# Two groups' small products in one run on TensorE, with four buffers each for their matrices and powers

## The chip, the cores and the metric

The kernel runs on one core of a Trainium2 chip. Its time is device microseconds of one execution, and the number that counts is the median of several. The core has five engines with a queue each: TensorE (PE in the profile; its weight loads have a row of their own, PEld), VectorE (DVE), ScalarE (ACT), GpSimd (POOL) and SyncE (SP, which here only issues transfers). Each engine works through its queue in order.

## The reference, cut to what matters

Two layers on 256 tokens of width 2048, in fp32. Each layer is a token mixer, a cross-attention to 256 memory tokens, and an MLP with a squared ReLU. Layer 1's mixer is a state space layer: 128 channel groups of 16 channels, each driving 64 complex states.

```
lam_bar = exp(lam * dt)
b_bar = ((lam_bar - 1.0) / lam)[..., None] * bmat
bu = einsum('gpc,bsgc->sbgp', b_bar, u)
_, states = associative_scan(combine, (a, bu), axis=0)
y = einsum('gcp,sbgp->bsgc', cmat, states).real + d_skip * u
...
def squared_relu_mlp(h, w_up, w_down):
    return jnp.square(jax.nn.relu(h @ w_up)) @ w_down
```

## The kernel before

**Large matmuls.** Weights come as tiles of 128 x 1024 floats through SyncE's queue (`wload`, L127) into four buffers `wraw`, with a fifth in the first MLP. ScalarE casts each to a high part `whi` (L103) and VectorE subtracts to get the low part `wlo` (L104); each of these has three buffers. TensorE multiplies high by high and low activations and low by high activations. In the MLP's up projection (`gemm_feat`, L174 and L179) a tile is eight matmuls of 512 columns and eight of 256; in the down projection (`gemm_hid`, L814, L815, L817) it is twelve of 512. The first MLP (`mlp`, layer 0) has four blocks of 32 up tiles and 32 down tiles.

**The state space preparation.** What the state space layer needs of its parameters doesn't depend on tokens. `ssm_prep` works it out during the first MLP. It puts small steps on a list `side`; every second tile, `tick` takes one step and traces it under `later(200)`, which lowers the priority of its instructions by 200 against the matmuls around them, so they stand later in the queues of the engines than where they were traced. The first steps work out the powers of the poles (`power`, tiles `pw`), transpose them (`spread`, L1026, to `T1` and `T2`) and write eight rows of factors to DRAM (`row`, `Ld`, L1014). Then come 32 "quads" of four channel groups, in three steps each:

- `quad(q)` loads the quad's matrices `bcq` (GpSimd) and half of its factors `lb` (SyncE, L1062) and makes the input matrix `bb` (L1077 to L1079), in one of two buffers.
- `quad_q(q)` loads the other half of `lb`, from `Ld`, makes the products of the output matrices and the powers, `qt` (L1087 to L1089, two buffers), sends them to DRAM (`Qd`), and multiplies `bb` by `qt` on TensorE: four matmuls, one per channel group, each with 32 columns of weights and 128 moving columns, into 32 partitions each of one PSUM tile `kp` (L1100). A matmul in fp32 leaves two records in the trace. ScalarE (L1104) and VectorE (L1105) copy `kp` to `kd`, of which GpSimd has cleared the first part (L1103), and GpSimd sends `kd` to DRAM in four transfers (`Kd`, L1108).
- `quad_p(q)` multiplies the factors to `po` (two buffers) and sends it to DRAM (`Pd`, L1122).

The four products carry a priority that makes up for their order, so that all four have the same one:

```
for g in range(4):
    with self.tc.high_priority(offset=g):
        nc.tensor.matmul(kp[32 * g:32 * g + 32], bb[:, g], qt[:, 0:T, g, :], start=True, stop=True,
                         skip_group_check=True)
```

**The next stage.** `s5` reads `Pd`, `Qd` and `Kd` back. It has runs of small matmuls of the same shape as the products above: `own` (L1215) and `outputs` (L1263, followed by L1269).

**Activation tiles.** `act` has two buffers of 128 x 8192 floats. In the first MLP one holds its input `hT`; the other, which held the attention's output, is idle until the norm of the next layer takes it in the last block (`nxt.start`).

Of the kernel before, what the change touches and what calls it, by code (L numbers as in the profile page):

```python
# [9 lines left out]
F32 = mybir.dt.float32  # L10
# [3 lines left out]
ALU = mybir.AluOpType  # L14
AX = mybir.AxisListType

P = 128
D = 2048
S = 256
KT = D // P  # L20
# [10 lines left out]
G = 128  # L31
T = 8
# [6 lines left out]
class Trunk:  # L39
# [590 lines left out]
    def mlp(self, x, layer, cur, nxt):  # L630
# [3 lines left out]
        with tc.tile_pool(name="ml", bufs=4, reuse_waits="tile") as mp:  # L634
            r2 = mp.tile([P, 32 if layer else 56], F32, name="r2", bufs=1)[:, 0:2]
            ws = lambda: mp.tile([P, KB * NB], F32, name="ws", bufs=4)
# [272 lines left out]
    def ssm_prep(self, pool):  # L909
# [14 lines left out]
        self.Qd = mk("Qd", [2, 64, 2, 4 * P])  # L924
        self.Kd = mk("Kd", [16, NL, 2, 4, 16])
        Ld = self.dram.tile([T, G, 2, 64], F32, name="Ld")
# [7 lines left out]
        F = pool.tile([P, 2, G], F32, name="F", bufs=1)  # L934
        e = {}

        def cmul(orr, oi, ar, ai, br, bi):
# [9 lines left out]
        def poles():  # L947
# [5 lines left out]
            nc.gpsimd.memset(T2[:, 0, :], 0.0)  # L953
            e["bb"] = [pool.tile([P, 4, 2, 16], F32, name=f"bb{i}") for i in range(2)]
            for b in e["bb"]:
                nc.gpsimd.memset(b[:, :, 1], 0.0)
            lr, li = pool.tile(W, F32, name="lr", tag="w0"), pool.tile(W, F32, name="li", tag="w1")
            ld = pool.tile([P, 1], F32, name="ld")
# [8 lines left out]
        def place(k):  # L967

            if k % 4 == 1:
                e["p4"] = pool.tile([P, 4, 2, P], F32, name="pw", tag="lb", bufs=2)  # L970
            e["pw"].append(tuple(e["p4"][:, (k - 1) % 4, i] for i in range(2)))
            return e["pw"][k]
# [77 lines left out]
        def inputs(q):  # L1050
            e["bcq", q] = bcq = pool.tile([P, 4, 4, 16], F32, name="bcq", bufs=3)
            nc.gpsimd.dma_start(out=bcq, in_=a["b_bc"][q])

        def factors(q, i):

            if i == 0:
                e["lb", q] = pool.tile([P, 2, 4, 2, 64], F32, name="lb", bufs=2)
            b = a["b_pc"][q]
            src = (bass.AP(tensor=b.tensor, offset=b.offset, ap=[[0, T], [8 * 64, 16], [1, 8 * 64]]),
                   bass.AP(tensor=Ld.tensor, offset=Ld.offset + q * 8 * 64, ap=[[G * 2 * 64, T], [0, 16], [1, 8 * 64]]))  # L1060
            with self.tc.issue_after(self.fed):
                nc.sync.dma_start(out=e["lb", q][:, i], in_=src[i])  # L1062

        def quad(q):
            factors(q, 0)
            bcq = e.pop(("bcq", q))
# [4 lines left out]
            B1, C2, B2, C1 = (bcq[:, i] for i in range(4))  # L1071
            bb = e["bb"][q % 2]
            tq = pool.tile([P, 4, T + 1, 16], F32, name="tq")
# [17 lines left out]
        def quad_q(q):  # L1091
            factors(q, 1)
            bcq, bb, tq = e[q]
            qt = pool.tile([P, T + 1, 4, 16], F32, name="qt", bufs=2)
            times(qt.rearrange("p w g c -> p g w c"), tq, T + 1, q, bcq[:, 3], bcq[:, 1])
            nc.gpsimd.dma_start(out=self.Qd[q // 2][q % 2].rearrange("p r n -> r p n"), in_=qt[:, 1:])
            kp = self.ps([P, T, 16])
            for g in range(4):
                with self.tc.high_priority(offset=g):
                    nc.tensor.matmul(kp[32 * g:32 * g + 32], bb[:, g], qt[:, 0:T, g, :], start=True, stop=True,  # L1100
                                     skip_group_check=True)
            kd = pool.tile([P, NL, 16], F32, name="kd", bufs=2)
            nc.gpsimd.memset(kd[:, 0:T - 1, :], 0.0)  # L1103
            nc.scalar.copy(out=kd[:, T:, :], in_=kp[:, 1:, :])  # L1104
            v.scalar_tensor_tensor(out=kd[:, T - 1, :], in0=eye, scalar=dsk[:, q:q + 1], in1=kp[:, 0, :],  # L1105
                                   op0=ALU.mult, op1=ALU.add)
            for t in range(4):
                nc.gpsimd.dma_start(out=self.Kd[q // 2][:, :, q % 2, t], in_=kd[32 * t:32 * t + 16])  # L1108

        def quad_p(q):  # L1110

            tq, lb = e.pop(q)[2], e.pop(("lb", q))
            bt = lb[:, 0]
            po = pool.tile([P, 4, 2, 64], F32, name="po", bufs=2)
            tmp = tq.rearrange("p a b c -> p (a b c)")[:, 0:512].rearrange("p (t r s) -> p t r s", t=4, r=2)
# [5 lines left out]
            v.tensor_tensor(out=po[:, :, 1], in0=po[:, :, 1], in1=tmp[:, :, 1], op=ALU.add)  # L1121
            nc.gpsimd.dma_start(out=self.Pd[q // 2][:, q % 2], in_=po.rearrange("p t r s -> p t (r s)"))  # L1122

        sd = self.side
# [3 lines left out]
        sd += [lambda k=k: power(k) for k in range(5, T + 1)]  # L1128
        sd += [lambda: spread(5), lambda: (last(), inputs(0))]
        for q in range(G // 4):  # L1130
# [6 lines left out]
    def s5(self, x, cur, nxt):  # L1137
# [3 lines left out]
        with tc.tile_pool(name="s5", bufs=2, reuse_waits="tile") as sp:  # L1141
# [110 lines left out]
            def outputs(n, half):  # L1252
# [4 lines left out]
                for i in (2 * half, 2 * half + 1):  # L1257
                    dq = ahead.pop(("dq", n, i)).rearrange("p (j l t c) -> p l t j c", j=T, l=2, t=4)
                    qq = ahead.pop(("qq", n, i))
# [283 lines left out]
```

## Time and profile before

| | us |
|---|---|
| median of 3 runs | 2790.95 |
| lowest, highest | 2790.82, 2792.07 |
| the profiled execution | 2789.63 |
| its span, first to last instruction | 2787.9 |
| TensorE matmuls busy | 2767.1 |
| VectorE busy | 1984.8 |
| ScalarE busy | 1396.2 |
| GpSimd busy | 234.4 |

The profile is of one execution, which is 1.3 us shorter than the median. Between its time and its span lie 1.7 us. Busy times are unions of the records of an engine; matmuls overlap each other in the records, since the end of one is modelled, so the distance from one start to the next tells more of TensorE than the busy share does.

### The profile page before, as it was taken

To read this page: it belongs to the slowest core of one execution; us is meant where nothing else is said; L and a number is where in the kernel's file an instruction comes from. 1 tells how busy PE (TensorE), PEld (TensorE's weight loads), DVE (VectorE), ACT (ScalarE), POOL (GpSimd) and SP (SyncE) were. 2 spreads that over 40 slices of the span, in tenths; PEclk is the share of its full clock that TensorE was granted. 3 is DMA by queue.
4 is the path that set the end of the run, shared out by engine and by line. 5 is a ranking of instruction groups with operands and counts; after the bars stand their busy time and mean duration, and the time that the engine had idled before them with its cause. 6 is when DMAs were issued, how large, how long until landed. Compare 5 with 4: busy or idle time off the path is not lost. (4 is left out here: it accounts for less than half of the span.)

```text
span 2787.9 us, 39690 instructions
## 1 busy us (share of the span) xinstructions
PE 2767.1 (99%) x15020; PEld 2331.6 (84%) x15020; DVE 1984.8 (71%) x2740; ACT 1396.2 (50%) x1805; POOL 234.4 (8%) x435
## 2 busy tenths in 40 slices
PE   9999999999999999999999999999999999999998
PEld 7888888888888888888887888888888888888887
DVE  6865756778978778787567657557776767667665
ACT  6545544554534434444556445445554545445454
POOL 0100000001022222221213100000000000000000
PEclk9999999999999999999999999999999999999999
DMA  8766655557788888887879767564556566565655
GB/s 294 232 209 217 200 179 181 175 158 244 211 260 260 255 259 262 257 259 226 240 242 270 217 199 239 176 191 159 179 158 216 170 212 204 164 221 167 213 187 158
DMA packets 196223, 593.76 MB, mean 213 GB/s; under 512 B 45120, under 2 KB 47216, under 8 KB 195520
## 3 DMA queue, kind: packets, MB, share of 16 engines
q1 hardware_dynamic: 151728, 531.17, 60.7%
q0 software_dynamic: 43776, 59.01, 7.8%
q8 instruction: 117, 1.92, 0.3%
q10 hardware_dynamic: 528, 1.06, 0.1%
q14 instruction: 74, 0.61, 0.1%
HBM read 567.51 MB, written 23.46 MB: 212 GB/s over the span
## 5 line engine op out<-in xcount | busy, mean ns | idle before, releaser
L104 DVE TENSOR_TENSOR wlo<-wraw,whi 128x1024 fp32r<-128x1024 f32 (+1 forms) x893 | 1085.9, 1221 | 490.4 <-ACT whi L103 484.8
L103 ACT CAST whi<-wraw 128x1024 fp32r<-128x1024 f32 (+1 forms) x893 | 937.3, 1052 | 857.0 <-PE acc L731 204.5
L174 PE MATMUL acc<-act,whi 128*128 128x512 f32 x3072 | 742.4, 392 | 0.6 <-ACT whi L103 0.6
L174 PEld LDWEIGHTS acc<-act,whi 128*128 128x128 f32 x3072 | 562.7, 188 | 111.5 <-issue 2.6
L179 PEld LDWEIGHTS acc<-act,wlo 128*128 128x128 f32 x3072 | 394.9, 191 | 18.6 <-DVE wlo L104 2.9
L179 PE MATMUL acc<-act,wlo 128*128 128x256 f32 x3072 | 403.9, 283 | 1.9 <-DVE wlo L104 1.5
L159 PE MATMUL acc<-whi,act 128*128 128x512 f32 x1472 | 369.8, 393 | 6.2 <-ACT whi L103 5.4
L159 PEld LDWEIGHTS acc<-whi,act 128*128 128x128 f32 x1472 | 275.1, 189 | 64.0 <-ACT whi L103 5.4
L731 PE MATMUL acc<-whi,act 128*128 128x512 f32 x864 | 233.0, 392 | 0.0
L815 PE MATMUL acc<-whi,hl 128*128 128x512 f32 x544 | 213.3, 392 | 0.0
L814 PE MATMUL acc<-whi,hh 128*128 128x512 f32 x544 | 212.7, 391 | 0.0
L159 PE MATMUL acc<-wlo,act 128*128 128x512 f32 x736 | 197.9, 391 | 0.0
L731 PEld LDWEIGHTS acc<-whi,act 128*128 128x128 f32 x864 | 160.3, 188 | 36.5 <-ACT ends L763 1.9
L159 PEld LDWEIGHTS acc<-wlo,act 128*128 128x128 f32 x736 | 138.6, 188 | 28.9
L731 PE MATMUL acc<-whi,hh 128*128 128x512 f32 x378 | 148.4, 393 | 0.0
L731 PE MATMUL acc<-whi,hl 128*128 128x512 f32 x378 | 147.1, 389 | 0.0
L817 PE MATMUL acc<-wlo,hh 128*128 128x512 f32 x544 | 145.9, 390 | 0.0
L731 PE MATMUL acc<-wlo,act 128*128 128x512 f32 x432 | 133.1, 390 | 0.0
L815 PEld LDWEIGHTS acc<-whi,hl 128*128 128x128 f32 x544 | 102.1, 188 | 23.1 <-issue 2.2
L190 ACT COPY r<-acc 128x512 f32<-128x512 f32 x64 | 37.6, 587 | 166.7 <-PE acc L174 166.7
L817 PEld LDWEIGHTS acc<-wlo,hh 128*128 128x128 f32 x544 | 102.1, 188 | 21.5 <-issue 0.2
L814 PEld LDWEIGHTS acc<-whi,hh 128*128 128x128 f32 x544 | 102.1, 188 | 21.4 <-issue 0.4
(369 smaller groups left out, 2762.4 us busy)
## 6 DMA issues: line engine op xcount, KB each, us to landing
wraw<-in_f_w_up SPq DMA_DIRECT2D x256, 512.0 KB, 4.6
wraw<-in_f_w_down SPq DMA_DIRECT2D x228, 512.0 KB, 4.6
wraw<-in_x_w_q SPq DMA_DIRECT2D x64, 512.0 KB, 4.1
wraw<-in_x_w_k SPq DMA_DIRECT2D x64, 512.0 KB, 4.4
wraw<-in_b_w_out SPq DMA_DIRECT2D x64, 512.0 KB, 4.4
wraw<-in_a_w_in SPq DMA_DIRECT2D x63, 512.0 KB, 4.1
wraw<-in_x_w_v SPq DMA_DIRECT2D x48, 512.0 KB, 4.2
wraw<-in_x_w_o SPq DMA_DIRECT2D x48, 512.0 KB, 4.3
```

The lines of the kernel that those rows point to most:

```text
L103: self.nc.scalar.copy(out=hi, in_=src)
L104: return self.nc.vector.tensor_tensor(out=lo, in0=src, in1=hi.bitcast(F32), op=ALU.subtract).ins
L159: nc.tensor.matmul(out[t], a[:, kt, sl], b[:, kk, :], start=st and a is ah, stop=en)
L174: nc.tensor.matmul(acc[:, f, :], hi[:, kk, sl], both[:, kt].rearrange("p a s -> p (a s)"), start=first and kk == 0, stop=last and kk == FK ...
L179: nc.tensor.matmul(acc[:, f, 0:S], lo[:, kk, sl], ah[:, kt, :], start=False, stop=last and kk == FK - 1, skip_group_check=True)
L190: nc.scalar.copy(out=dst, in_=acc[:, :, S:])
L731: mm = lambda s, m, e: nc.tensor.matmul(out, s, m, start=key not in begun, stop=e, skip_group_check=True)
L814: nc.tensor.matmul(acc[:, t, :], ah, hi[:, kk, :], start=kt == 0, stop=False)
L815: nc.tensor.matmul(acc[:, t, :], al, hi[:, kk, :], start=False, stop=False)
L817: nc.tensor.matmul(acc[:, t, :], hid[kt // 4][0][:, kt % 4, sl], lo[:, kk, :], start=False, stop=kt == KT - 1)
```

## The change

Every two quads (a pair) now do their products together, in the second one's `quad_q`: eight matmuls into one PSUM tile of twice the size, with a priority that makes up for the order of all eight; then one copy by ScalarE and two by VectorE into a `kd` of twice the size. The transfers of `kd` to DRAM come four a pair instead of four a quad, with runs of 32 floats instead of 16 in a new layout of `Kd`, and are issued after the next pair's first `Pd`. The cleared part of `kd` is cleared once for each of two buffers. `bb`, `qt` and `po` have four buffers each, `kd` two, all in one tile `room` that takes the idle activation buffer. The factors `lb` are loaded one quad earlier, in three buffers, which they share with the powers `pw`. A filler in the MLP's pool gets smaller. The reading side follows the new layout.

```diff
@@ mlp
-            r2 = mp.tile([P, 32 if layer else 56], F32, name="r2", bufs=1)[:, 0:2]
+            r2 = mp.tile([P, 32 if layer else 24], F32, name="r2", bufs=1)[:, 0:2]
@@ ssm_prep
-        self.Kd = mk("Kd", [16, NL, 2, 4, 16])
+        self.Kd = mk("Kd", [16, NL, 4, 2, 16])
...
+        room, used = self.act.tile([P, 2 * KT * S], F32, name="room", tag="act"), [0]
+
+        def home(n):
+            used[0] += n
+            return room[:, used[0] - n:used[0]]
+
+        bbs = [home(4 * 2 * 16).rearrange("p (g k c) -> p g k c", g=4, k=2) for _ in range(4)]
+        qts = [home((T + 1) * 4 * 16).rearrange("p (w g c) -> p w g c", g=4, c=16) for _ in range(4)]
+        pos = [home(4 * 2 * 64).rearrange("p (t r s) -> p t r s", t=4, r=2) for _ in range(4)]
+        kds = [home(NL * 2 * 16).rearrange("p (w i c) -> p w i c", i=2, c=16) for _ in range(2)]
@@ poles
-            e["bb"] = [pool.tile([P, 4, 2, 16], F32, name=f"bb{i}") for i in range(2)]
-            for b in e["bb"]:
+            for b in bbs:
                 nc.gpsimd.memset(b[:, :, 1], 0.0)
+            for k in kds:
+                nc.gpsimd.memset(k[:, 0:T - 1], 0.0)
@@ place
-                e["p4"] = pool.tile([P, 4, 2, P], F32, name="pw", tag="lb", bufs=2)
+                e["p4"] = pool.tile([P, 4, 2, P], F32, name="pw", tag="lb", bufs=3)
@@ factors
-                e["lb", q] = pool.tile([P, 2, 4, 2, 64], F32, name="lb", bufs=2)
+                e["lb", q] = pool.tile([P, 2, 4, 2, 64], F32, name="lb", bufs=3)
@@ quad
-            factors(q, 0)
+            if q + 1 < G // 4:
+                factors(q + 1, 0)
...
-            bb = e["bb"][q % 2]
+            bb = bbs[q % 4]
@@ quad_q
-            factors(q, 1)
+            if q + 1 < G // 4:
+                factors(q + 1, 1)
             bcq, bb, tq = e[q]
-            qt = pool.tile([P, T + 1, 4, 16], F32, name="qt", bufs=2)
+            qt = qts[q % 4]
...
-            kp = self.ps([P, T, 16])
-            for g in range(4):
-                with self.tc.high_priority(offset=g):
-                    nc.tensor.matmul(kp[32 * g:32 * g + 32], bb[:, g], qt[:, 0:T, g, :], start=True, stop=True,
-                                     skip_group_check=True)
-            kd = pool.tile([P, NL, 16], F32, name="kd", bufs=2)
-            nc.gpsimd.memset(kd[:, 0:T - 1, :], 0.0)
-            nc.scalar.copy(out=kd[:, T:, :], in_=kp[:, 1:, :])
-            v.scalar_tensor_tensor(out=kd[:, T - 1, :], in0=eye, scalar=dsk[:, q:q + 1], in1=kp[:, 0, :],
-                                   op0=ALU.mult, op1=ALU.add)
+            if q % 2:
+                products(q // 2)
+
+        def products(m):
+
+            kp = self.ps([P, 2, T, 16])
+            for i in range(2):
+                bb, qt = bbs[2 * (m % 2) + i], qts[2 * (m % 2) + i]
+                for g in range(4):
+                    with self.tc.high_priority(offset=4 * i + g):
+                        nc.tensor.matmul(kp[32 * g:32 * g + 32, i], bb[:, g], qt[:, 0:T, g, :], start=True, stop=True,
+                                         skip_group_check=True)
+            kd = kds[m % 2]
+            nc.scalar.copy(out=kd[:, T:].rearrange("p w i c -> p i w c"), in_=kp[:, :, 1:, :])
+            for i in range(2):
+                q = 2 * m + i
+                v.scalar_tensor_tensor(out=kd[:, T - 1, i, :], in0=eye, scalar=dsk[:, q:q + 1], in1=kp[:, i, 0, :],
+                                       op0=ALU.mult, op1=ALU.add)
+
+        def respond(m):
             for t in range(4):
-                nc.gpsimd.dma_start(out=self.Kd[q // 2][:, :, q % 2, t], in_=kd[32 * t:32 * t + 16])
+                nc.gpsimd.dma_start(out=self.Kd[m][:, :, t], in_=kds[m % 2][32 * t:32 * t + 16])
@@ quad_p
-            po = pool.tile([P, 4, 2, 64], F32, name="po", bufs=2)
+            po = pos[q % 4]
...
+            if q % 2 == 0 and q:
+                respond(q // 2 - 1)
+            if q == G // 4 - 1:
+                respond(q // 2)
@@ the list of side steps
-        sd += [lambda: spread(5), lambda: (last(), inputs(0))]
+        sd += [lambda: spread(5), lambda: (last(), inputs(0), factors(0, 0), factors(0, 1))]
@@ outputs
-                    dq = ahead.pop(("dq", n, i)).rearrange("p (j l t c) -> p l t j c", j=T, l=2, t=4)
+                    dq = ahead.pop(("dq", n, i)).rearrange("p (j t l c) -> p l t j c", j=T, l=2, t=4)
```

## Rows read from the trace of the kernel before

**Rows 1.** The page, part 1: busy us (share of the span) and instructions.

```profile
PE 2767.1 (99%) x15020; PEld 2331.6 (84%) x15020; DVE 1984.8 (71%) x2740; ACT 1396.2 (50%) x1805; POOL 234.4 (8%) x435
```

**Rows 2.** Busy times by stretch: PE, PEld, DVE, ACT, POOL, granted clock, DMA share, GB/s.

```profile
780.00:1330.00 550.00, 550.00 (x2964) 457.97 (x2963) 439.41 (x655) 237.59 (x281) 138.16 (x255) 1.00 0.85 252
...
1392.00:1600.00 208.00, 205.50 (x1853) 164.84 (x1852) 145.75 (x295) 116.37 (x199) 43.66 (x75) 1.00 0.81 244
```

**Rows 3.** Timeline of TensorE, down projection: start, duration, what.

```profile
1014.29 0.39 PE L814 MATMUL acc<-whi,hh 128*128 128x512 f32 x1
...
1017.01 0.39 PE L814 MATMUL acc<-whi,hh 128*128 128x512 f32 x1
...
1017.79 0.42 PE L1100 MATMUL ps<-qt,bb 128*32 128x128 f32 x8
1018.14 0.50 PE L815 MATMUL acc<-whi,hl 128*128 128x512 f32 x1
...
1020.32 0.39 PE L814 MATMUL acc<-whi,hh 128*128 128x512 f32 x1
```

**Rows 4.** Waits of TensorE, whole span: us in total, times, longest.

```profile
PE acc L179 <- DVE wlo L104: 1.5, 3, 0.5
```

**Rows 5.** Line 1100 alone: durations in ns, first and last start.

```profile
L1100 PEld LDWEIGHTS ps<-qt,bb x256: 106/108/109, 780.4 to 1322.5; 128*32 128x32 f32 x128
L1100 PE MATMUL ps<-qt,bb x256: 272/285/297, 780.4 to 1322.6; 128*32 128x128 f32 x128
```

**Rows 6.** Timeline of TensorE, up projection.

```profile
1075.69 2.00 PE L174 MATMUL acc<-act,whi 128*128 128x512 f32 x8
1077.63 0.43 PE L1100 MATMUL ps<-qt,bb 128*32 128x128 f32 x8
...
1079.93 2.08 PE L179 MATMUL acc<-act,wlo 128*128 128x256 f32 x16
1081.85 3.82 PE L174 MATMUL acc<-act,whi 128*128 128x512 f32 x16
1085.50 2.08 PE L179 MATMUL acc<-act,wlo 128*128 128x256 f32 x16
```

**Rows 7.** Timeline of TensorE, state space stage.

```profile
1428.40 1.95 PE L1215 MATMUL ps<-pq,us 128*32 128x128 f32 x64
1430.28 2.11 PE L159 MATMUL acc<-whi,act 128*128 128x512 f32 x8
...
1459.35 0.64 PE L1263 MATMUL ps<-dq,us 128*32 128x128 f32 x16
1459.93 0.58 PE L1269 MATMUL ps<-qq,vv 64*32 64x128 f32 x24
```

**Rows 8.** Line 1089 alone, the instruction that completes `qt`.

```profile
L1089 DVE TENSOR_TENSOR qt<-qt,tq x32: 748/751/759, 761.9 to 1287.7; 128x576 f32<-128x576 f32 x32
```

**Rows 9.** Waits from 690 to 1395 us, of all engines.

```profile
ACT whi L103 <- PE acc L815: 177.2, 116, 1.7
...
DVE bb L1077 <- PE ps L1100: 17.0, 13, 1.8
...
ACT whi L103 <- DMA wraw<-in_f_w_up: 3.5, 3, 2.6
```

**Rows 10.** Timeline of SyncE's queue.

```profile
742.92 0.62 SPq L1062 DMA_DIRECT2D lb<-Ld  x1
```

**Rows 11.** Line 1014 alone, the rows of `Ld`: issues, and time to landing.

```profile
L1014 POOL DMA_DIRECT2D Ld<-lk x7: 537/537/550, 701.7 to 739.0; - x7
...
DMA to landing us min/median/max: 2.1/2.5/4.1
```

**Rows 12.** DMA issues from 690 to 1395 us: KB, median us to landing.

```profile
wraw<-in_f_w_down SPq DMA_DIRECT2D x128, 512.0 KB, 6.0
```

**Rows 13.** Timeline of TensorE during `spread(5)`.

```profile
756.21 0.27 PE L1026 MATMUL ps<-ident,pw 128*128 128x128 f32 x1
756.24 0.48 PE L814 MATMUL acc<-whi,hh 128*128 128x512 f32 x1
...
758.64 0.27 PE L1026 MATMUL ps<-ident,pw 128*128 128x128 f32 x1
```

## The prediction

> **What bounds the kernel now.** I read the page's busy line first: TensorE's matmuls cover 99% of the span, VectorE 71%, ScalarE 50%, GpSimd 8% [rows 1]. The change lies in the first MLP, where the state space preparation runs beside the weight stream, so I then asked for that stretch alone: from 780 to 1330 us the matmuls are busy for all 550.00 us, at a granted clock of 1.00 [rows 2]. A busy matmul row alone proves little, because matmul records overlap, so I went to the timeline and looked at starts. In the down projection a tile of twelve 512-column matmuls takes 2.72 us (1014.29 to 1017.01), back to back with nothing between [rows 3]. TensorE waits for nothing there: of its waits in the whole span, the largest for VectorE's `wlo` add up to 1.5 us, in three pieces [rows 4]. So in this stretch the end of the kernel moves by what TensorE's own queue gets shorter or longer, and by nothing else, as long as the others stay ahead.
>
> [...]
>
> **What one group costs.** The change joins the small products of two groups of four channels ("quads"). The trace has 256 matmul records of line 1100, which come eight at a time, so 32 groups [rows 5]. A group's price is read by comparing tiles. In the down projection the tile that holds one lasts from 1017.01 to 1020.32, 3.31 us, against 2.72 without: 0.59 us [rows 3]. In the up projection a pair of tiles with a group lasts 1075.69 to 1079.93, 4.24 us, and without one 1081.85 to 1085.50, 3.65 us: again 0.59 us [rows 6]. All 32 together: 18.9 us.
>
> How much of this is the work and how much the change over from the large matmuls and back? The state space stage has matmuls of the same form (128 rows, 32 columns of weights, 128 columns moving) in longer runs. Sixty-four records in a row take from 1428.40 to 1430.28, 1.88 us, until the next instruction starts; eight of line 1100 take 1017.79 to 1018.14, 0.35 us [rows 3, 7]. So eight more records cost (1.88 - 0.35) / 7 = 0.22 us. A run of sixteen agrees: 1459.35 to 1459.93, 0.58 us, which is 0.23 more than eight [rows 7]. The other 0.59 - 0.22 = 0.37 us are paid once a group, whatever its length.
>
> **What the change removes and adds.**
> *Products.* The same 128 matmuls now come as 16 groups of sixteen records. A group then costs 0.59 + 0.22 = 0.81 us, with the bound of the sixteen-run 0.82, against 2 x 0.59 = 1.18: saved 0.36 to 0.37 us, sixteen times, 5.8 to 5.9 us. I take 5.8, by the run of the same length. Nothing hides this on TensorE: it is the queue itself that gets shorter.
>
> [...]
>
> *Does TensorE wait for the second quad?* A pair's products stand behind `qt` of its second quad, as a single's now stand behind its own. The first `qt` is done at 761.9 + 0.75 us and its products start at 780.4; the last is done at 1288.5 and its products start at 1322.5 [rows 5, 8]. So the cover is at least 17.7 us, and I put the wait at nothing; if VectorE fell behind by more than that, each further microsecond would be one on the path.
>
> *Four buffers instead of two.* VectorE waits 17.0 us, in 13 pieces, for the products before it may overwrite `bb` [rows 9]. With two pairs of buffers it has to wait only for the pair before last. That stall goes, and the weight splits behind it on VectorE come earlier. TensorE does not wait for them now, so the gain is nothing in time. ScalarE copies the result, with weight casts behind each copy; there will be half as many copies, each twice as wide. The casts wait for TensorE to free their buffer (177.2 us in 116 pieces) and for the weights' transfer only 3.5 us in three [rows 9], so they are not the late ones, and this too is nothing.
>
> *GpSimd.* The 128 transfers of `kd` become 64 of twice the run length, and the memset before each goes. GpSimd is 8% busy [rows 1], and TensorE first reads what these transfers bring at 1459.35, in the next stage [rows 7]. Nothing. The transfers are issued later (behind the next pair's first `Pd`), and the last pair's directly after the last `Pd`.
>
> *SyncE.* The factor loads go one quad earlier, into a third buffer, so most get a longer lead at the same number of transfers. The first quad's `lb<-Ld` is traced two side steps earlier, four weight tiles. It is issued at 742.92 now, so by the steps alone it could reach the head of the queue at 742.92 - 4 x 2.72 = 732.0 us [rows 3, 10]. It reads the last row of `Ld`, which GpSimd sends at 739.0 and which lands 2.5 us later (at most 4.1), so at 741.5 to 743.1 [rows 11]. SyncE, with weight loads behind this one, would stand between nothing and 11.1 us. I take the lower part, some 2.5 us, as the load can't be queued before the transfer that it depends on is. The cover: five weight buffers at 2.72 us each make a cycle of 13.6 us, of which a load takes 6.0 from issue to landing [rows 12]; the other 7.6, and two tiles (5.4 us) that are already converted, make 13.0 us, less a cast and a split. So nothing on TensorE; without that cover the 2.5 us would be on the path, once.
>
> *The idle activation tile.* `room` takes the buffer that the attention's output used, and it is free when the MLP starts; the next norm then takes the buffer of the MLP's input, which the last up projection has finished reading eight tiles (21.8 us) before the first write. `yT` takes `room` in the next stage, and is first written behind the small products that start at 1428.40, when the last use of `room` by TensorE (1322.5) is long over [rows 5, 7]. Nothing.
>
> **Sum.** The profiled execution took 2789.63 us with a span of 2787.9; less 5.8 gives a span of 2782.1 and 2783.8 us. The median of the runs shown is 2790.95, 1.3 above the profiled one, so the time is 2790.95 - 5.8 = 2785.1 us. A difference of 0.2% is 5.6 us (about what a measurement of this kernel can tell from no change), so this sits just beyond that line, at 0.21%.
>
> **Rivals.**
> *Loads in the open (same).* If the second quad's weight loads are not hidden, each of its two rounds of four pays one load of 0.108 us more [rows 5]: a pair costs 0.81 + 0.22 = 1.03, saved 0.15 x 16 = 2.4, time 2788.6. Against it stands the run of sixty-four.
> *Nothing gained (same).* If a pair's eight products fall into two runs of four again, the fixed 0.37 us are paid 32 times as now: 2790.9.
> *The group falls apart (slower).* Side work stands in the queues by priority. Transposes of the preparation that are given no common priority come one by one between large matmuls: eight of them, from 756.21 to 758.64, each with one large matmul behind it [rows 13]. The products are held together by an offset that grows by one per matmul, and the new one runs over eight instead of four. If a pair came in three pieces, it would pay 0.37 three times: 16 x 0.37 = 5.9 us more than now, 2796.9. It turns from gain to loss beyond two pieces. Against it: the same device holds four together in the groups shown, with x8 in one row [rows 3, 6].
> *More than the groups (faster).* If VectorE's freed 17.0 us also shorten TensorE's waits, they can do so only outside this stretch, which has none. The next stage has 208.00 - 205.50 = 2.5 us without a matmul [rows 2]; if most of it went, the time would be 2783.2.
>
> **How the numbers follow.** The sum as worked out 0.75, with a range of its own from 2784.2 to 2786.2; loads in the open 0.05; nothing gained 0.06; falls apart 0.06; more than the groups 0.08. The range from 2783.2 to 2788.6 takes in the first, second and last, 0.88. The line of 0.2% is at 2785.4, inside the first case; I put 0.48 of its 0.75 beyond it. Faster: 0.48 + 0.08 = 0.56; same: 0.27 + 0.05 + 0.06 = 0.38; slower 0.06.
>
> **What would show it.** Sixteen rows of x16 for the products, each some 0.57 us to the next large matmul, and a down tile with one lasting about 3.53 us; no wait of VectorE's `bb` for the products; 64 issues of `Kd`; the stretch of the first MLP shorter by 5.8 us and all later stages as long as before. The prediction is wrong if products come as x8 rows still, if TensorE shows waits for `qt`, if SyncE's early `lb<-Ld` starves the casts near 740 us, or if the 5.8 us come back as waits in the next stage.

## The result, and the profile after

The changed kernel took 2783.38 us (median of 10 runs, 2782.36 to 2785.84); the kernel before, on the same chip, 2790.89 us (10 runs, 2788.78 to 2795.37). The ratio is 0.9975, with a 95% interval of 0.9967 to 0.9984: faster by 7.5 us, 0.25%. The profiled execution took 2782.36 us, 7.27 less than the one before.

The page's busy line, against [rows 1]: TensorE has as many instructions and 7.0 us less busy time, and GpSimd issues less.

```profile
PE 2760.1 (99%) x15020; PEld 2332.5 (84%) x15020; DVE 1984.8 (71%) x2740; ACT 1394.9 (50%) x1789; POOL 191.5 (7%) x343
```

The products now stand on line 1120. This is TensorE's timeline in the down projection and in the up projection, against [rows 3, 6] (start, duration, what):

```profile
1012.83 0.39 PE L814 MATMUL acc<-whi,hh 128*128 128x512 f32 x1
...
1013.60 0.64 PE L1120 MATMUL ps<-room 128*32 128x128 f32 x16
1014.17 0.50 PE L815 MATMUL acc<-whi,hl 128*128 128x512 f32 x1
1014.51 0.40 PE L814 MATMUL acc<-whi,hh 128*128 128x512 f32 x1
...
1014.99 0.40 PE L814 MATMUL acc<-whi,hh 128*128 128x512 f32 x1
...
1016.38 0.40 PE L814 MATMUL acc<-whi,hh 128*128 128x512 f32 x1
...
1019.11 0.39 PE L814 MATMUL acc<-whi,hh 128*128 128x512 f32 x1
...
1036.68 3.82 PE L174 MATMUL acc<-act,whi 128*128 128x512 f32 x16
...
1041.62 0.65 PE L1120 MATMUL ps<-room 128*32 128x128 f32 x16
...
1043.01 3.82 PE L174 MATMUL acc<-act,whi 128*128 128x512 f32 x16
...
1048.58 3.59 PE L174 MATMUL acc<-act,whi 128*128 128x512 f32 x15
```

The reader is to see x16 where x8 stood, 0.57 us from the first small product to the next large matmul, and a down tile of 3.55 us (1012.83 to 1016.38) where the next one, without products, takes 2.73 (3.53 and 2.72 by the prediction). In the up projection the pair with a group takes 6.33 us (1036.68 to 1043.01), and the next 5.57.

To have each run's price I went through the starts of the matmuls in the trace and took, for every run of small products, what the large matmuls around it came late against their usual spacing (0.2267 us for 512 columns). A run of sixteen costs 0.78 to 0.84 us, the sixteen of them 13.12 us; before, a run of eight cost 0.58, the 32 of them 18.55 us. That is 5.43 us.

The same starts, cut into stages, say where the 7.27 us lie. The cuts are at the first transposes (line 236) for the MLP, its first down projection (814), the first product with `b_w_in` (159) and the 400th behind that, the first of line 174 after it, and the first of line 731; all in us:

```
          opening  first up  preparation  400 of b_w_in    to 174    to 731   to the end
before     662.39     91.10       637.62         115.03    193.85    192.60       895.33
after      661.23     90.71       632.13         114.97    193.83    192.48       895.29
```

The preparation stage gives 5.49 us, as much as the runs do. A seam ahead of it gives 0.39. In that seam a stand of TensorE of 0.4 us (at 693.4, for `wlo`) is gone; it is gone in joined_late below as well, which has none of the new buffers, so it isn't shown to be the change's. The opening, in which no line was changed, gives 1.16; it is 660.8 to 662.8 us in the profiles of all kernels of this study, so this is taken for the scatter of single executions. Behind the preparation nothing moved by more than 0.12 us. The windows to [rows 2] (columns as there) agree:

```profile
780.00:1330.00 550.00, 550.00 (x2988) 464.47 (x2987) 442.70 (x655) 237.47 (x268) 101.83 (x173) 1.00 0.82 256
1392.00:1600.00 208.00, 205.44 (x1849) 164.91 (x1849) 142.54 (x281) 114.19 (x191) 43.61 (x75) 1.00 0.82 242
```

The waits between 690 and 1395 us, against [rows 9] (us in total, times, longest), and TensorE's own in the whole span, against [rows 4]:

```profile
ACT whi L103 <- DMA wraw<-in_f_w_down: 11.8, 5, 3.4
...
DVE room L1089 <- PE ps L1120: 0.4, 1, 0.4
```

```profile
PE acc L179 <- DVE wlo L104: 1.2, 3, 0.5
```

VectorE's wait for the products, 17.0 us before, is down to 0.4. ScalarE's casts wait for a weight transfer more often than before (11.8 us in five), and no TensorE wait comes of it. SyncE's early load of `Ld` is issued at 741.90, against 742.92 in [rows 10], and the queue goes on behind it at once:

```profile
741.90 0.62 SPq L1073 DMA_DIRECT2D lb<-Ld  x1
742.62 0.40 SPq L127 DMA_DIRECT2D wraw<-in_f_w_down  x1
```

### The profile page after: what moved, and what is told of

Its sections match the earlier page's. It is cut to its first block, busy times and chain, and to the rows that moved or that the text cites. A ratio compares the mean times of both kernels' runs of the same rounds, so it can differ in the third digit from the quotient of the medians.

```text
span 2780.7 us, 39458 instructions
## 1 busy us (share of the span) xinstructions
PE 2760.1 (99%) x15020; PEld 2332.5 (84%) x15020; DVE 1984.8 (71%) x2740; ACT 1394.9 (50%) x1789; POOL 191.5 (7%) x343
```

## The experiments

The theory on trial is the prediction's: each change from large to small products and back has a price of its own, and the change pays it 16 times and no more 32 times. The rivals: the gain comes from the room (four buffers, early factors, `Kd` in pairs) that frees VectorE and GpSimd; and any joining of products pays, however it is done. "The stage" is the preparation stage of the table above. All medians come with the ratio to the kernel before, on the same chip.

### Is it the changeover?

**apart** keeps all of the change but issues each quad's four products in its own step, again 32 runs of eight records.

```
         def quad_q(q):
...
+            for g in range(4):
+                with self.tc.high_priority(offset=g):
+                    nc.tensor.matmul(kp[32 * g:32 * g + 32, q % 2], bb[:, g], qt[:, 0:T, g, :], ...)
             if q % 2:
-                products(q // 2)
+                products(q // 2, kp)
```

> All of the change stays (four buffers in the idle activation tile, early factors, one copy and four transfers a pair), but each quad's four products run by themselves, in their own quad's step, so that there are 32 runs of eight records again instead of 16 of sixteen. Theory 'changeover' (the gain is what TensorE pays once a run, 0.34 us): 16 x 0.34 = 5.5 us slower than the changed kernel, about 2789, and within 2 us of the kernel before. Rival 'freed engines' (VectorE's 17 us of waits, GpSimd's and the small writes' share of the gain): 2784 to 2786, at least half of the gain stays.

Measured: 2788.94 us, ratio 0.9992 (0.9983 to 1.0000); the stage takes 637.62 us, as before to the hundredth. The room alone gives nothing in the stage; in the whole it is 1.9 us by the medians, with an interval from nothing to 4.7, so a small gain outside the stage is neither shown nor excluded. The 5.5 us need the joint runs.

**no_offset** goes the other way: the offsets in priority that hold the eight products of a pair together are left away.

```
-                    with self.tc.high_priority(offset=4 * i + g):
-                        nc.tensor.matmul(kp[32 * g:32 * g + 32, i], bb[:, g], qt[:, 0:T, g, :], ...)
+                    nc.tensor.matmul(kp[32 * g:32 * g + 32, i], bb[:, g], qt[:, 0:T, g, :], ...)
```

> The changed kernel without the offsets in priority that keep the small products of a pair together: the eight products of a pair are placed by the planner one at a time between large ones. Theory (each run of small products between large ones costs some 0.35 us over its own work, whatever its length): eight runs per pair instead of one, 16 x 7 x 0.35 = 39 us more than the changed kernel, about 2822 us. Rival (it is the number of small products that costs, not the changes): about 2783 us.

Measured: 2834.33 us (two runs), ratio 1.0154 (1.0136 to 1.0173); the stage takes 679.37 us, 47.2 more than in the changed kernel, and TensorE waits for no other engine in it. The 256 records come in 112 runs, 105 of them a single product (two records). TensorE's timeline:

```profile
954.11 0.41 PE L1119 MATMUL ps<-room 128*32 128x128 f32 x2
954.44 0.49 PE L814 MATMUL acc<-whi,hh 128*128 128x512 f32 x1
954.87 0.41 PE L1119 MATMUL ps<-room 128*32 128x128 f32 x2
```

A large matmul and a lone product together take 0.76 us (954.11 to 954.87) where the large one alone takes 0.227: 0.53 us for two records, nearly as much as for eight. It is the number of runs that costs. The theory had the direction and undersized it, 47 us against 39: my fixed 0.35 us a run is too little for the shortest runs (47.2 / 96 further runs = 0.49).

### What is the room for?

**two_buffers** keeps the joint products with two buffers each of `bb` and `qt`.

```
-        bbs = [home(4 * 2 * 16)... for _ in range(4)]
-        qts = [home((T + 1) * 4 * 16)... for _ in range(4)]
+        bbs = [home(4 * 2 * 16)... for _ in range(2)]
+        qts = [home((T + 1) * 4 * 16)... for _ in range(2)]
...
-            bb = bbs[q % 4]
+            bb = bbs[q % 2]
```

> The products stay together, but bb and qt have two buffers instead of four, so the next pair's first bb has to wait until TensorE has done this pair's products. Theory 'changeover': the sixteen runs stay, so TensorE's own queue is as in the changed kernel, 2783.4; VectorE's wait for the products, 0.4 us in the changed kernel, grows to well over the 17 us of the kernel before, and the time rises only if that wait outlasts the converted weights in store. Rival 'freed engines': the gain hangs on VectorE's waits, so with waits above 17 us the time is that of the kernel before or worse, 2790 and more.

Measured: 2785.22 us, ratio 0.9976 (0.9966 to 0.9986); the stage again 632.13 us. The waits between 690 and 1395 us:

```profile
DVE bcq L1082 <- DMA bcq<-in_b_bc: 10.9, 5, 3.4
...
DVE room L1089 <- PE ps L1120: 2.4, 3, 1.0
```

I had thought that VectorE's 17 us would grow; they shrank to 2.4, since its queue now brings the next two `bb` behind the joint products. Four buffers of these two are not what the gain needs, as long as `Po` has four: VectorE works in bursts here (nine times it finishes two `Po` 5.6 to 7.1 us apart; in the changed kernel they are never less than 9.8 apart), and it doesn't wait for `Po`'s buffers.

**late_factors** takes the factor loads back into their own quad's steps, and with that `lb` and `pw` to two buffers.

```
-            if q + 1 < G // 4:
-                factors(q + 1, 0)
+            factors(q, 0)
...
-                e["lb", q] = pool.tile([P, 2, 4, 2, 64], F32, name="lb", bufs=3)
+                e["lb", q] = pool.tile([P, 2, 4, 2, 64], F32, name="lb", bufs=2)
```

> The changed kernel with the factor loads where they were before (in their own quad's steps) and two buffers for them and the powers. Theory 'changeover': no difference, 2783.4 within 1 us. Rival 'the early factors do part of it' (the 1.5 us between what the runs of products account for and the measured gain): 1 to 2 us slower, 2784.5 to 2785.5.

Measured: 2789.12 us, ratio 0.9993 (0.9985 to 1.0002), yet the stage is 632.13 us as in the changed kernel. The loss lies behind it: the 400 products with `b_w_in` take 121.29 us and not 114.97. GpSimd's timeline, then TensorE's, then the windows:

```profile
1324.63 0.62 POOL L1177 DMA_DIRECT2D pq<-Pd  x1
1387.10 1.59 POOL L1177 DMA_DIRECT2D pq<-Pd  x3 [61.84 <-issue]
```

```profile
1422.18 1.97 PE L1226 MATMUL ps<-ident,u 128*128 128x128 f32 x8 [3.53 <-ACT u L1215]
1423.80 3.76 PE L159 MATMUL acc<-whi,act 128*128 128x512 f32 x8
1427.36 1.24 PE L159 MATMUL acc<-wlo,act 128*128 128x512 f32 x4
```

```profile
1400.00:1420.00 20.00, 18.64 (x83) 15.10 (x81) 10.61 (x14) 9.37 (x19) 6.44 (x11) 1.00 1.05 250
1420.00:1440.00 20.00, 17.82 (x130) 14.82 (x131) 9.01 (x11) 11.71 (x20) 2.10 (x4) 0.83 0.83 283
```

The next stage's reads of `Pd`, which go out between 1322 and 1325 us in the changed kernel, stand for 62 us on something until 1387, and then share the DMA engines with the first weights of `b_w_in` (DMA share 1.05); the casts wait for those weights (13.0 us in five pieces, from 1385 to 1430 us), TensorE waits 3.5 us, and in the window behind that its granted clock is 0.83 (below). Either the late loads themselves did that, or the smaller pool: with one buffer less, the tiles of the next stage lie elsewhere in the memory, over buffers still in use. **late_three** tells these apart: factors late, but three buffers, so that the pool is as large as in the changed kernel.

> The changed kernel with the factors recorded in their own quad's steps (as in the run late_factors), but with the three buffers of lb and pw kept, so that the pool of the stage is as large as in the changed kernel. Theory (the 6.3 us that late_factors lost at the start of the first layer with state-space terms came from where the next stage's tiles lie, so that their loads wait longer): the stretch from the first products with b_w_in to 400 matmuls on is 115.0 us as in the changed kernel, GpSimd's first load of pq is issued near 1325, and the whole is 2783.4 us (2782 to 2785). Rival (factors recorded early are themselves worth those microseconds): that stretch is some 121 us again and the whole is 2789. In both the preparation stage is 632.1 us.

Measured: 2784.40 us, ratio 0.9978 (0.9969 to 0.9987); the stage 632.13, the 400 products 114.93 us. GpSimd's timeline:

```profile
1323.63 2.22 POOL L1177 DMA_DIRECT2D pq<-Pd  x4
```

So the early factors are worth nothing that can be measured, and the third buffer matters only by its size. Which buffer the second `pq` waited for was not traced. In the profile of late_three the stretch behind the 400 products is 3.3 us longer than in the changed kernel's (197.15 us against 193.83); TensorE stands 1.6 us for a load there, and the median is 1.0 us above the changed kernel's, inside the scatter.

**joined_only** starts from the kernel before and joins the products alone.

```
-            kp = self.ps([P, T, 16])
+            if q % 2:
+                kp = self.ps([P, 2, T, 16])
+                for i in range(2):
+                    for g in range(4):
+                        with self.tc.high_priority(offset=4 * i + g):
+                            nc.tensor.matmul(kp[32 * g:32 * g + 32, i], e["bb"][i][:, g], ...)
+                for i in range(2):
+                    respond(q - 1 + i, kp[:, i])
```

> The kernel before with nothing changed but that the products of two quads are issued together, sixteen... that is two times eight records with no large product between them, into two parts of one PSUM tile; two buffers of bb and qt as before, kd copied quad by quad, factors in their own steps, Kd as before. Theory (the whole gain is the changeover): the preparation stage falls from 637.6 to about 632.1 us and the whole to about 2785.4 us, 5.5 less than before, unless bb or qt, which now both live until the joint run, hold VectorE back for longer than its slack. Rival (the four buffers or the layout of Kd are needed for it): 2789 to 2791 us.

Measured: 2807.27 us (five runs; the profiled one is the longest, 2813.72), ratio 1.0060 (1.0047 to 1.0073): the theory as I had stated it fell, by 22 us. The sixteen runs of sixteen are there, at 13.13 us in all, so TensorE's own gain was had in full. But the stage takes 660.13 us. A row of the waits between 690 and 1395 us, TensorE's own in that stretch, the timelines of GpSimd and of VectorE, and a window:

```profile
DVE po L1125 <- DMA Pd<-po: 46.9, 9, 9.0
```

```profile
PE acc L179 <- DVE wlo L104: 10.4, 6, 3.6
PE acc L817 <- DVE wlo L104: 7.0, 3, 3.2
```

```profile
996.62 0.58 POOL L1129 DMA_DIRECT2D Pd<-po  x1 [0.38 <-DVE bcq L1070]
...
1030.31 4.50 POOL L1115 DMA_DIRECT2D Kd<-kd  x8 [26.97 <-DVE bb L1077]
```

```profile
995.91 0.42 DVE L1128 TENSOR_TENSOR po<-po,tq 128x256 f32<-128x256 f32 x1
...
1001.95 0.42 DVE L1128 TENSOR_TENSOR po<-po,tq 128x256 f32<-128x256 f32 x1
1010.47 0.69 DVE L1125 TENSOR_TENSOR po<-lb 128x512 f32<-128x512 f32 x1 [8.10 <-DMA Pd<-po]
```

```profile
1000.00:1020.00 20.00, 17.23 (x64) 13.63 (x63) 10.04 (x14) 5.26 (x5) 2.11 (x4) 0.83 0.80 247
```

Eight transfers of `Kd` stand for 27 us at the head of GpSimd's queue, because the products that they wait for come later now. They don't hold back `Po`, though: the `Po` that VectorE finishes at 996.33 goes out at 996.62. In all nine of VectorE's waits its transfer goes out 0.3 to 0.9 us after VectorE has finished it. The rest is the way to DRAM, about as long as in the kernel before; the time from issue to landing of `Po`'s 32 transfers, before (L1122) and in joined_only (L1129):

```profile
DMA to landing us min/median/max: 5.9/9.7/14.9
DMA to landing us min/median/max: 5.3/10.4/14.7
```

What has changed is when VectorE wants the buffer back. With two buffers each of `bb` and `qt`, its work for both next quads stands behind the joint products, and it finishes two `Po` 6 us apart (996.33 and 1002.37); nine times in the stage it is 5.6 to 7.1 us, where before it was never less than 10.7. The third `Po` then needs the buffer of the first, and VectorE waits up to 9.0 us for that transfer to land; the splits of the weights stand behind it in VectorE's queue, and TensorE waits for `wlo`. From the starts of the matmuls: 18.4 us of standing, and 9.5 us more by which the large matmuls behind such stands came late against their usual spacing (granted clock 0.83 in the window). 632.1 + 18.4 + 9.5 = 660.0.

What of the room prevents that? **kd_early** undoes the place of `Kd`'s transfers: they are recorded right behind a pair's products and no more two quads later.

```
                                       op0=ALU.mult, op1=ALU.add)
+            respond(m)
...
-            if q % 2 == 0 and q:
-                respond(q // 2 - 1)
-            if q == G // 4 - 1:
-                respond(q // 2)
```

> The changed kernel with one thing undone: a pair's four transfers of Kd are given to GpSimd at once behind its products, as in the kernel before, and no more two quads later behind Po's. Theory (joined_only lost 22 us in the stage because the transfers of Kd wait in GpSimd's queue for the late joint products, and the loads and transfers behind them, above all Po's, hold VectorE): GpSimd waits at Kd for some ten or more us a time, VectorE's wait for Po's buffers or for bcq reaches wlo, and the stage takes 636 to 655 us, the whole 2788 to 2806 us. Rival (the four buffers of bb, qt and Po give enough slack for that): the stage stays at 632.1 us and the whole at 2783 to 2785 us; what joined_only lacked is then the buffers of Po.

Measured: 2785.83 us, ratio 0.9978 (0.9969 to 0.9987), the stage 632.13 us. It tells little, since the order of GpSimd's queue did not follow the record; the planner put the transfers where they were. Changed kernel, then kd_early:

```profile
1010.69 0.56 POOL L1145 DMA_DIRECT2D Pd<-room  x1 [5.12 <-DVE room L1144]
1015.67 2.27 POOL L1131 DMA_DIRECT2D Kd<-room  x4 [4.43 <-issue]
```

```profile
1010.30 0.56 POOL L1146 DMA_DIRECT2D Pd<-room  x1 [5.13 <-DVE room L1145]
1015.30 2.28 POOL L1132 DMA_DIRECT2D Kd<-room  x4 [4.43 <-issue]
```

**joined_late** is joined_only with the eight transfers recorded two quads later.

```
+        def give(q):
+            for t in range(4):
+                nc.gpsimd.dma_start(out=self.Kd[q // 2][:, :, q % 2, t], in_=e["kd", q % 2][32 * t:32 * t + 16])
...
         def quad_p(q):
...
+            if q % 2 == 0 and q:
+                give(q - 2), give(q - 1)
```

> joined_only with one thing more: the eight transfers of a pair's Kd are given to GpSimd two quads later, behind the next pair's first Po, as in the changed kernel; two buffers each of bb, qt, kd and Po, factors in their own steps. Theory (the place of Kd's transfers in GpSimd's queue cost joined_only its 22 us): the stage falls from 660 to 632 to 634 us and the whole to 2784 to 2787 us. Rival (two buffers of Po and the late factors are too few when the products are joined): the stage stays above 640 us and the whole above 2793 us.

Measured: 2801.45 us, ratio 1.0039 (1.0027 to 1.0052), the stage 648.32 us: better by 12, not cured. The waits between 690 and 1395 us:

```profile
POOL kd L1110 <- DMA Kd<-kd: 114.6, 18, 9.4
...
DVE po L1129 <- DMA Pd<-po: 36.3, 12, 7.3
```

The place of the transfers is part of it; by what path wasn't traced. GpSimd's zero fills of `kd` now wait for the transfers, and VectorE still waits for `Po`'s. **kd_only** takes the changed kernel's pair-wide `kd` (zeros written once, half the transfers) and undoes all other room: two buffers each of `bb`, `qt` and `Po`, factors late, with the pool's size kept.

```
-        pos = [home(4 * 2 * 64)... for _ in range(4)]
+        pos = [home(4 * 2 * 64)... for _ in range(2)]
...
-            po = pos[q % 4]
+            po = pos[q % 2]
```

(with the edits of two_buffers and late_three)

> The changed kernel with all of its room undone except kd's: two buffers each of bb, qt and Po, the factors in their own steps (in the three buffers of the changed kernel, so that the next stage's tiles lie as there); kept are the joint products, the pair-wide kd (zeros written once, one copy, four transfers for a pair). joined_late, which has kd quad by quad with a zero fill and eight transfers for a pair, took 648 us for the stage. Theory (GpSimd's queue, held up by kd's zero fills and by twice as many transfers, held the transfers of Po back, and VectorE with them: the pair-wide kd is what the joint products need): the stage takes 632 to 633 us and the whole 2783 to 2786 us. Rival (two buffers of Po are too few with joint products): VectorE waits some 30 us for Po's transfers as in joined_late, and the stage takes 640 to 650 us, the whole 2791 to 2802 us.

Measured: 2793.20 us, ratio 1.0009 (1.0000 to 1.0018), the stage 639.75 us. The rival holds. VectorE's waits:

```profile
DVE room L1139 <- DMA Pd<-room: 39.1, 7, 7.3
```

The stage is 8.6 us shorter than joined_late's, and the wait for `Po`'s transfers remains, though each goes out 0.3 us after VectorE has finished its `Po`. With four buffers of `Po`, two of `bb` and `qt` (two_buffers) or late factors (late_three) cost the stage nothing, so here the two buffers of `Po` make the wait. But they make it only together with VectorE's bursts, which are those of two_buffers (again nine times 5.7 to 7.1 us). The kernels of the next section have two of `Po` and eight of `bb` and `qt`; VectorE finishes `Po` at least 13 us apart there and never waits for its transfers. In the changed kernel's trace every transfer of `Po` has landed 15 us or more before VectorE starts the `Po` after the next, so by my estimate two would do there too; that was not run. By these runs joint products need room in one of the two places.

### Could fewer runs give more?

**four_quads** joins four quads: eight runs of 32 records.

```
-            if q % 2:
-                products(q // 2)
+            if q % 4 == 3:
+                products(q // 4)
...
-            kp = self.ps([P, 2, T, 16])
-            for i in range(2):
+            kp = self.ps([P, 4, T, 16])
+            for i in range(4):
```

(eight buffers of `bb` and `qt`, two of `Po`, one `kd` of four quads' width)

> Four quads' products in one run of 32 records, eight runs in all, with eight buffers of bb and qt, two of po and one kd, in the same tile. Theory 'changeover': 8 x 0.34 = 2.7 us less than the changed kernel, 2780.7, and 24 x 0.34 = 8.2 less than before. Rival 'freed engines': VectorE's waits are gone already, so nothing more, 2783.4, or slower, since GpSimd's transfers of kd now come in bursts of eight from a single buffer and po has two buffers only.

Measured: 2792.34 us, ratio 1.0006 (0.9997 to 1.0015), the stage 637.39 us. TensorE's timeline:

```profile
903.62 1.08 PE L1120 MATMUL ps<-room 128*32 128x128 f32 x32
```

A run of 32 costs 1.23 us, the eight of them 9.83: 3.3 us less than sixteen of sixteen, somewhat more than the 2.7 that eight changeovers at 0.34 would give. It was lost again to 6.2 us of TensorE standing and 2.4 us by which the matmuls behind that came late. The longest stand follows VectorE's longest wait for the load of `bcq` (8.2 us at 931.2; 43.2 us in 17 pieces in all). I blamed the bursts of eight `Kd` transfers in GpSimd's queue. **four_spread** gives them four at a time, as the change does.

```
             if q % 2 == 0 and q > 2:
                 respond(q // 2 - 2)
```

> Eight runs of 32 products, as in four_quads, but with the sixteen transfers of a run's Kd and Po given to GpSimd in the same portions as in the changed kernel (four of Kd at a time, one portion behind every second quad) instead of eight at once. Theory (the changeover between large and small products costs some 0.35 us each time, and four_quads lost it again because the load of bcq stood behind bursts of transfers in GpSimd's queue): TensorE's waits for wlo in the stage fall from 6.7 us to about the changed kernel's level, the stage is 629.4 to 630.5 us, and the whole 2780.7 to 2782 us. Rival (the wait comes from the single buffers of kd, po and bcq, not from the burst): the stage stays at 634 to 638 us and the whole at 2785 to 2790.

Measured: 2793.75 us, ratio 1.0008 (0.9999 to 1.0017), the stage 641.97 us: the theory of the bursts fell. **four_ahead** also records the load of `bcq` one quad earlier, in the same three buffers.

```
-            if q + 1 < G // 4:
-                inputs(q + 1)
+            if q + 2 < G // 4:
+                inputs(q + 2)
```

> four_spread (eight runs of 32 products) with the load of bcq recorded one quad earlier, in the same three buffers. In four_spread VectorE stood 7.9 us for a bcq that had been issued 10 us before it landed, and TensorE then waited for wlo. Theory (that wait is all that covers the gain of fewer runs): VectorE's wait for bcq all but goes, the stage takes 629.4 to 630.5 us and the whole 2780.7 to 2782.5 us. Rival (another queue takes its place: the two buffers of Po, or GpSimd's waits): TensorE still waits for wlo and the stage stays above 634 us, the whole above 2785 us.

Measured: 2793.20 us, ratio 1.0008 (0.9999 to 1.0017), the stage 637.23 us. A row of VectorE's waits and one of GpSimd's, then the timelines of GpSimd, VectorE and TensorE:

```profile
POOL bcq L1063 <- DVE tq L1100: 134.5, 24, 19.5
DVE room L1089 <- DMA bcq<-in_b_bc: 43.7, 16, 7.7
```

```profile
918.49 0.82 POOL L1109 DMA_DIRECT2D Qd<-room  x1 [5.64 <-DVE room L1101]
919.30 0.60 POOL L1063 DMA_DIRECT2D bcq<-in_b_bc  x1
```

```profile
929.60 0.23 DVE L1089 TENSOR_TENSOR room<-F,bcq 128x64 f32<-128x64 f32 x1 [7.72 <-DMA bcq<-in_b_bc]
```

```profile
931.61 3.78 PE L179 MATMUL acc<-act,wlo 128*128 128x256 f32 x16 [3.71 <-DVE wlo L104]
```

The wait is as long as without the edit: the load is issued no earlier, behind a transfer of `Qd` at 918.49, and it landed 10 us later, when the median is 5.1; VectorE has it next in its queue. GpSimd's row says why an earlier line may not help: with three buffers of `bcq`, GpSimd stands at 24 of these loads until VectorE's line 1100 has read the old contents. More buffers of `bcq` were not tried. So the rival's forecast holds here too, by GpSimd's waits and not by the two buffers of `Po`. A version with eight runs and without that wait might give some 3 us more; none of the three is one, and none beats the change.

## Why the prediction was right

**The fixed price of a run.** Right, and shown by taking it away and putting it back (apart 637.62, joint 632.13, single 679.37 us). The terms were some hundredths off: the sixteen-run 0.82 us on the mean, which is the bound that I gave beside 0.81; the eight-run 0.58 on the mean, where one tile and one pair had shown 0.59. So the saving is 0.34 us a pair and not 0.36, and the stage 5.5 us shorter and not 5.8.

A run of two records costs 0.53 us (no_offset), nearly what one of eight does (0.58). What in the engine takes that time isn't shown by any row.

**Loads in the open.** Excluded: eight more records add 0.24 us from eight to sixteen and 0.20 a time from sixteen to 32, loads and all. In four_quads' run the matmuls start in rounds of four, 0.109 us apart (903.754, 903.863, 903.972), and a load lasts 0.106 to 0.110 us (the changed kernel's line 1120): two rounds, each as long as a load, make the eight records, with the matmuls beside the loads. **Nothing gained** and **the group falls apart**: neither came, as all sixteen rows are x16. The price of falling apart was too low in my working (0.37 us a piece; 0.49 in no_offset).

**More than the groups.** Excluded as I priced it: the stretch of the next stage has 205.44 us of matmul in 208 against 205.50. The time is nevertheless 1.7 us below the forecast, and 0.8 us below the range that I gave the sum for itself (2784.2 to 2786.2); the stage alone came 0.3 us short of the forecast saving. That the time still lies in the wide range, whose lower end is this rival's price, is luck, since this rival's mechanism did not come. By the profile the seam ahead of the preparation gave 0.4 us beside the stage, and the opening 1.2. Three more kernels have the same stage of 632.13 us and no loss of late_factors' kind behind it (two_buffers 2785.22, late_three 2784.40, kd_early 2785.83); with the change their mean is 2784.7, and the forecast of 2785.1 lies among them. I take the rest for scatter; nothing shows a cause.

**What I costed at nothing.** TensorE never waits for the second quad's `qt` (none of its waits for another engine in the changed kernel's whole span is at line 1120), and GpSimd's and SyncE's parts are hidden: `lb<-Ld` is issued at 741.90, by the ordering that I had taken (behind the landing of the last `Ld` at 741.75), and the queue goes straight on. The early factors cost and bring nothing (late_three). The price of four buffers was right as a sum and wrong as a picture. I looked at VectorE's wait for `bb`, which all but went even with two buffers, and at TensorE's cover for the second `qt`, which held even in joined_only. What joint products endanger is a path that I had not named: with two buffers of `bb` and `qt` VectorE's work for two quads comes in one burst behind the products, and with two of `Po` it then waits for the transfer of the first `Po`, and the split of the weights behind that. The joint products alone made the kernel 16 us slower, and I had no rival for it, because I costed the parts one by one against a kernel that has them all.

## What to carry to other kernels

Count how often a busy TensorE changes between its large matmuls and small products of another tile shape: here each run cost some 0.35 to 0.5 us over its own work (0.34 us saved a pair by the change, 0.49 lost a run in no_offset), and joining runs was worth that on TensorE each time. But a joint run gives its operands' buffers back all at once, so the engine that fills them may begin to work in bursts (here two `Po` 5.6 to 7.1 us apart, nine times in joined_only, where before it was never less than 10.7). Look at every other buffer that this engine fills within a burst, and whether its transfer has landed before the buffer is wanted again; more buffers at either place can cure it (here four of `Po` in two_buffers, with a stage of 632.13 us; with eight of `bb` and `qt` and two of `Po`, VectorE never waited for `Po`'s transfers). And where a planner orders the queues, moving a line in the program may move nothing, as in kd_early: look at the order in the trace before you read the time.

## What the runs showed of the hardware

**A stand cost more than itself.** TensorE's granted clock is 1.00 from 780 to 1330 us of the changed kernel. In late_factors it stands 3.53 us; behind that eight 512-column matmuls take from 1423.80 to 1427.36, 0.445 us each and not 0.227, and the window from 1420 to 1440 us shows a granted clock of 0.83. By the starts, late matmuls behind stands cost some 9.5 us over 18.4 us of standing in joined_only, 2.4 over 6.2 in four_quads, and 4 over 11.5 in joined_late.

**Behind a short stand the clock fell in one profile and not in another.** Behind the same waits of 1.2 and 0.8 us in the next stage the clock stayed at 1.00 in the profile of the change, and was 0.96 over 40 us in that of kd_early, whose stretch behind the 400 products took 195.39 us and not 193.83. The windows, changed kernel first:

```profile
1500.00:1540.00 40.00, 37.67 (x403) 29.31 (x402) 31.39 (x71) 20.30 (x34) 16.96 (x29) 1.00 0.95 240
```

```profile
1500.00:1540.00 40.00, 37.71 (x395) 29.15 (x394) 31.07 (x70) 19.38 (x33) 19.02 (x32) 0.96 0.93 242
```

That is about 1.6 us of difference between single executions at one place, about as much as the forecast missed by; whether it is part of that miss isn't shown.

**Behind a run of small products the large matmuls came late for a while.** In no_offset's pattern two records cost 0.53 us, nearly what eight do; and behind a run of sixteen some of the next large matmuls come 0.235 to 0.24 us apart, as from 1014.51 to 1014.99 in the first timeline above, before they are back at 0.227.
